# A Delta-net layer and two convolutional FFNs on one core: new prices in the planner, and a second product that runs four places later

## The chip, the core and the metric

The program runs on one core of a Trainium2 chip. The core has a matrix engine (TensorE, PE in the profile; PEld is its weight load), three engines for element-wise work (VectorE = DVE, ScalarE = ACT, GpSimd = POOL), and a sync engine (SyncE = SP) whose queue issues most of the DMA transfers. POOL issues the transfers that add to what lies in memory. The metric is the device time of one execution, in microseconds (us). Each engine and each queue works its instructions in the order in which they stand in the program, and waits where an input is not ready.

## The reference

The model is a residual trunk of two layers on 1024 positions by 1024 channels, float32 throughout.

- Layer 0, attention part: `h = h + gated_deltanet(rmsnorm(h))`. A projection to q, k, v, z and two gates, a causal convolution of four taps with SiLU on q, k, v, then for 8 heads a chunked delta rule: inside a chunk a triangular system is solved, from chunk to chunk a state is carried, so that the chunks of a head follow one another. The output is normalised per head, multiplied with SiLU(z) and projected.
- Layer 1, attention part: chunked softmax attention over a key band, with a learned bias per head.
- After each of them: `h = h + conv_ffn(rmsnorm(h))`, that is

```
h = causal_dwconv(xn @ w_up, conv_w) + conv_b      # 1024 -> 5632 channels, three taps
gate, val = h[..., :2816], h[..., 2816:]
return (silu(gate) * val) @ w_down                 # 2816 -> 1024
```

- A final rmsnorm.

## The kernel before, in words

Every float32 factor of a product is cut into a high part that the PE reads exactly and a low rest (`hi`, `lo`), and a product is three matmuls: hi·hi, hi·lo, lo·hi. ACT copies the high part (`uh`, `dh`, `eh`), POOL or DVE subtracts it for the low part (`ul`, `dl`, `el`). Activations lie with channels on the partitions, 128 at a time, in two halves of 512 positions.

**Delta net (up to some 680 us).** The order in which instructions are emitted comes from a planner, the class `Flow`. It keeps a model of time `wv.T` that advances with each matmul group, and for each of DVE, ACT and POOL the time at which that engine is free: `wv.on("D", 1.3)` says that 1.3 us of work have just been emitted for DVE and returns when it will be done. Each piece of work (`gram`, `prep`, `merge`, `chain`, `finish`, `gate`, `yz`) is a generator that yields the time at which its next matmul can go. When none is due the planner emits an eighth of a dense projection tile (0.69 us in its model). A piece has a rank; among those that are due the lowest goes first, and ranks of 2 and more are held back when DVE or ACT is more than 4 us behind. So the prices in `wv.on` decide where each small matmul stands between the dense ones, and the PE then follows that order and waits where the model was too hopeful. Small tiles of 512 columns that live shortly (`th`, `yo`, `zt`, `sq`, `ez`) share two buffers under the tag `zt`.

**FFN (twice, from some 680 and some 1920 us).** The 22 tiles of the first product (one `val` and one `gate` block of 128 channels each) are made by a scheme with seven products of half-size matrices instead of eight (Strassen's): per tile `j` products 1, 7, 6, 5, 2, 4, 3, each 12 matmuls of 128x512 into a PSUM bank `pu`. Before a product, `left_sum` adds weight blocks (`r<-r,r` on DVE) and `operand` cuts them (`uh`, `ul`) two places ahead; after it, `after` puts the bank into `keep`, `keep7`, `vpre`, `gpre`. Then come three taps of `val` and three of `gate` (`taps`: the first on ACT, L1548; the others on DVE, L1551), `silu`, and `gated` (val times gate). Product 4 adds to the bank of product 7, so it may start only when `keep7` has read that bank.

The second product takes the hidden tiles in nine groups `g` of two, again with seven products (`second`, bank `pd`), whose results are drained into `stage` and added to DRAM by accumulating transfers (`drain`, `send`; one quarter first goes to `d_e`, which `load_e` and `send_e` add to three others at the end). The last four tiles, 18 to 21, are multiplied directly (`pf`), with weights `fr` that `load_last` loads and `cut_last` cuts, from hidden tiles that `hidden` cuts (`hidh`, `hidl`).

All of this stands in one list `seq` of PE steps, here called places. `at(i, f, rank)` puts the work `f` of the other engines ahead of place `i`; within a place, lower ranks come first. `pos[j, s]` is the place of the `s`-th product of tile `j`, `pos["d", g, n]` that of a product of group `g`, `end` the last product of tile 21, and `fin_at` the last product of the last group. When layer 1 finishes, its residual is loaded as `res` (`load_r`) and the sums as `ht` (`load_t`); in layer 0 they are `h`.

The attention between the two FFNs is not touched.

Of the kernel before, what the change touches and what calls it, by code (L numbers as in the profile page):

```python
# [9 lines left out]
F32 = mybir.dt.float32  # L10
# [8 lines left out]
KT = 8  # L19
# [9 lines left out]
def trunk_kernel(  # L29
# [541 lines left out]
    with ExitStack() as ph:  # L571
# [43 lines left out]
        soo, ff, rr = gt("soo"), gt("ff"), gt("rr")  # L615
# [23 lines left out]
        def split_tile(raw):  # L639
            wt = split_w(raw, [P, KT, P])  # L640
            wv.on("A", 1.0)
            return wt
# [24 lines left out]
        def project(m, dsts, key, store=None, n_from=0):  # L667
# [4 lines left out]
            def post(s, ps):  # L672
# [16 lines left out]
                def silu():  # L689
                    th = dp.tile([P, HALF], F32, name="th", tag="zt", bufs=2)  # L690
                    nc.scalar.activation(th, d, AF.Tanh)
                    nc.gpsimd.tensor_scalar(th, th, 1.0, 1.0, op0=ALU.add, op1=ALU.mult)
                    nc.gpsimd.tensor_tensor(d, d, th, op=ALU.mult)
# [44 lines left out]
        def gram(t):  # L738
# [11 lines left out]
            def decay(i):  # L750
                hd, E = hds[i], Es[i]
                nc.vector.tensor_tensor(E, E, negm.rearrange("p (o t) -> p o t", o=1).broadcast_to([P, 4, P]), op=ALU.add)
                yield wv.on("D", 0.75) - wv.slack
# [4 lines left out]
                yield wv.on("A", 1.4)  # L758
# [4 lines left out]
            for i, hd in enumerate(hds):  # L763
# [27 lines left out]
                slot[0] = t_ = wv.on("D", 1.3)  # L791
# [10 lines left out]
            wv.mark(("scale", t), wv.on("D", 1.2))  # L802
# [48 lines left out]
        def invert_blocks(t):  # L851
# [167 lines left out]
        def finish(t, j):  # L1019
# [18 lines left out]
            t_ = wv.on("D", 1.3)  # L1038
# [8 lines left out]
        def turn(k, s, vv):  # L1047
# [5 lines left out]
            yo = dp.tile([P, HALF], F32, name="yo", tag="zt", bufs=2)  # L1053
# [51 lines left out]
        def yz(k, s):  # L1105
# [11 lines left out]
            yield wv.on("D", 0.7) - wv.slack  # L1117
# [4 lines left out]
        def split_yt(yt, s, k):  # L1122
# [6 lines left out]
            wv.mark(("act", k, s), wv.on(e, 0.7 if e == "D" else 1.3, t))  # L1129

        def gate_z(hd):
            def post(s, ps):
                zt = dp.tile([P, HALF], F32, name="zt", tag="zt", bufs=2)
# [48 lines left out]
        def gates(gT):  # L1182
# [9 lines left out]
            ez = dp.tile([P, HALF], F32, name="ez", tag="zt", bufs=2)[:, 0:136].rearrange("p (c j) -> p c j", j=8)  # L1192
# [84 lines left out]
        env["tmp"] = lambda: dp.tile([P, HALF], F32, name="sq", tag="zt", bufs=2)  # L1277
# [28 lines left out]
        def out_tile(m, s):  # L1306
# [19 lines left out]
            def then():  # L1326
# [4 lines left out]
                wv.on("D", 0.65, wv.on("A", 0.65))  # L1331
# [8 lines left out]
            wv.later(wv.on("D", 0.6), then)  # L1340
# [25 lines left out]
        with tc.manual_schedule(engines={mybir.EngineType.PE, mybir.EngineType.DVE, mybir.EngineType.Activation}):  # L1366
# [20 lines left out]
            for n, (k, s) in enumerate([(k, 0) for k in range(8)] + [(k, 1) for k in range(4)]):  # L1387
                wv.add(3, ("yz", n % 6), wv.when(*[("gram", hd, 1) for hd in range(4, 8)]), yz(k, s))
# [29 lines left out]
    def ffn(layer, h, hp, xs, tail, d_r, last):  # L1418
# [215 lines left out]
        for c, (j, n) in enumerate(plan):  # L1634
# [3 lines left out]
            for g in range(NG):  # L1638
                for n, o in zip(ORDER, (2, 3, 5, 6, 8, 9, 11) if g == 0 else (-2, 0, 2, 4, 6, 8, 10)):
# [4 lines left out]
        for i, (j, n) in due.items():  # L1644
# [37 lines left out]
        for j in range(3, FP - 1):  # L1682
# [5 lines left out]
            0: [(11, (g0,), 0), (12, (v0,), 0), (13, (v1,), 2), (13, (v2,), 2.7), (15, (g1, g2, silu), 2), (17, (gated,), 2)],  # L1688
            1: [(18, (v0, v1), 2), (19, (v2, g0), 2), (20, (g1,), 2), (21, (g2, silu), 2), (22, (gated,), 2)],
            2: [(24, (v0, v1), 2), (25, (v2, g0), 2), (26, (g1,), 2), (27, (g2, silu), 2), (28, (gated,), 2)],  # L1690
        }
        for j in range(3, FP - 1):
            when[j] = [(pos[j, 7], (v0, v1), 2), (nx(j, 1), (v2, g0), 2), (nx(j, 2), (g1,), 2)]
            when[j] += [(nx(j, 3), (g2,), 2), (nx(j, 4), (silu,), 1.6), (nx(j, 5), (gated,), 2)]
            if j >= 2 * NG:
                when[j].append(({18: fin_at + 5, 19: fin_at + 7}.get(j, nx(j, 6)), (hidden,), 1.9))
# [135 lines left out]
        last_at = [pos[FP - 1, s] for s in (3, 4, 5, 6)] + [end + 1] * 4  # L1832
        if layer == 1:
            last_at = [pos[FP - 1, 2]] + last_at[:-1]
            last_at[5] = end
            last_at[7] = end + 2
# [21 lines left out]
        for q in range(8):  # L1858
            s = (1, 1, 2, 3, 4, 4, 5, 6)[q]
            at(fin_at + 1 if q < 2 else pos[FP - 1, s], lambda q=q: load_last(q), 1)  # L1860
            at(last_at[q], lambda q=q: cut_last(q), 1.5)

        if layer == 0:
# [55 lines left out]
        else:  # L1919
# [58 lines left out]
            for t in range(4):  # L1978
                step(("f", t, 0), tile_of(t, range(3)))
            for t in range(4):  # L1980
                step(("f", t), tile_of(t, range(3, 4)))
# [431 lines left out]
```

## Time and profile before

| | |
|---|---|
| median of 3 runs | 2588.57 us (2588.05 to 2591.74) |
| the profiled execution, own time | 2588.85 us |
| its span in the profile | 2587.0 us |
| PE busy | 2506.2 us, 13933 matmuls |
| DVE busy | 1861.0 us |
| POOL busy | 1476.3 us |
| ACT busy | 1414.3 us |

The span runs from the first to the last instruction of the program. A row of the view of stretches gives the bounds, the length, then busy time and number of instructions of PE, PEld, DVE, ACT and POOL, the granted PE clock (1.00 is full speed), the share of the 16 DMA engines and their rate. In the timeline a row is start, duration, engine, line, operation, and in brackets the idle time before it and what ended it. In the view of waits a row is the waiting instruction, what it waited for, the total in us, how often and the longest.

### The profile page before, as it was taken

The page shows a single profiled execution, that of the slowest core. Times are in us where ns is not written, and L with a number is a line of the kernel's source. Part 1 is how long each engine was busy: PE and PEld are TensorE (multiplying, and loading weights), DVE is VectorE, ACT ScalarE, POOL GpSimd, SP SyncE. Part 2 cuts the span into 40 slices and gives each one's busy share as a digit, 9 for nine tenths or more (in the row PEclk, how much of TensorE's full clock was granted, in tenths as well). Part 3 has the DMA queues.
Part 4 walks back from the last instruction along what each step waited for, and adds up shares of the span by engine and source line. Part 5 has one row for each costly group of instructions (what it writes and reads, how often), then busy time and mean ns, then how long its engine had stood idle before and what let it go on. Part 6 is the DMA issues. An engine that isn't in the chain of part 4 may idle for free.

```text
span 2587.0 us, 39395 instructions
## 1 busy us (share of the span) xinstructions
PE 2506.2 (97%) x13933; PEld 2068.8 (80%) x13933; DVE 1861.0 (72%) x3102; ACT 1414.3 (55%) x2735; POOL 1476.3 (57%) x1466
## 2 busy tenths in 40 slices
PE   7999999999999999999999999999999999999988
PEld 5878788888877888888788888887876788888877
DVE  5765864554588888888876666666488788888875
ACT  6444455464455555655556555565455655565553
POOL 3655543345437777777726444443433777777770
PEclk9999999999999999999999999999999999999999
DMA  4534435555436777777841211113332576777785
GB/s 128 139 100 118 127 101 161 147 166 156 121 82 135 147 144 153 156 153 152 173 157 54 65 52 56 45 50 100 104 97 79 138 151 143 154 155 150 158 190 174
DMA packets 320598, 325.15 MB, mean 126 GB/s; under 512 B 32912, under 2 KB 244624, under 8 KB 320400
## 3 DMA queue, kind: packets, MB, share of 16 engines
q1 hardware_dynamic: 289584, 219.59, 29.0%
q0 software_dynamic: 25920, 94.38, 20.5%
q10 hardware_dynamic: 4896, 8.65, 1.0%
q8 instruction: 110, 1.80, 0.3%
q14 instruction: 88, 0.72, 0.1%
HBM read 179.89 MB, written 142.67 MB: 125 GB/s over the span
## 4 chain that ended last, share of the span: by engine, by line
PE 54%; DVE 6%; POOL 3%; issue 3%; ACT 2%; DMA 1%; DVEq 0%; ACTq 0%; POOLq 0%
PE pu L1458 8%; PE pu L1456 8%; PE pu L1457 8%; PE pd L1458 4%; PE pd L1457 4%; PE pd L1456 4%; PE acc L119 3%; PE acc L120 3%; PE acc L121 3%; PE ptp L2137 2%; POOL ul L1423 2%; PE sc L2109 1%; PE poT L2167 1%; PE poT L2166 1%; PE sc L2110 1%
## 5 line engine op out<-in xcount | busy, mean ns | idle before, releaser
L1423 POOL TENSOR_TENSOR ul<-r,uh 128x512 fp32r<-128x512 f32 x282 | 445.4, 1598 | 304.9 <-ACT uh L1444 280.9
L119 PE MATMUL acc<-xh,whi 128*128 128x512 f32 x896 | 375.4, 419 | 0.2
L120 PE MATMUL acc<-xl,whi 128*128 128x512 f32 x896 | 354.0, 395 | 2.0 <-POOL xl L421 1.0
L121 PE MATMUL acc<-xh,wlo 128*128 128x512 f32 x896 | 352.7, 394 | 0.0
L1444 ACT CAST uh<-r 128x512 fp32r<-128x512 f32 x296 | 181.7, 623 | 218.0 <-DVE r L1423 176.8
L104 POOL TENSOR_TENSOR wlo<-wraw,whi 128x256 fp32r<-128x256 f32 (+2 forms) x206 | 169.4, 851 | 159.1 <-ACT whi L102 139.3
L1456 PE MATMUL pu<-xh,uh 128*128 128x512 f32 x552 | 216.0, 391 | 2.8 <-ACT uh L1444 1.3
L1458 PE MATMUL pu<-xh,ul 128*128 128x512 f32 x552 | 215.7, 391 | 1.7 <-POOL ul L1423 1.7
L1457 PE MATMUL pu<-xl,uh 128*128 128x512 f32 x552 | 215.5, 390 | 1.0 <-POOL xl L421 1.0
L1778 ACT COPY stage<-pd 128x1024 f32<-128x1024 f32 x180 | 174.8, 1013 | 49.4 <-PE pd L1458 49.4
L121 PEld LDWEIGHTS acc<-xh,wlo 128*128 128x128 f32 x896 | 168.9, 189 | 37.3
L120 PEld LDWEIGHTS acc<-xl,whi 128*128 128x128 f32 x896 | 170.2, 190 | 25.5 <-DVE xl L1163 3.2
L119 PEld LDWEIGHTS acc<-xh,whi 128*128 128x128 f32 x896 | 169.9, 190 | 21.7 <-ACT xh L1162 1.1
L2117 POOL TENSOR_SCALAR sS<-sS,st 128x640 f32<-128x640 f32 (+4 forms) x128 | 85.3, 668 | 172.4 <-DVE st L2116 125.2
L1551 DVE SCALAR_TENSOR_TENSOR val<-vpre,colt,val 128x1023 f32<-128x1023 f32 (+2 forms) x92 | 152.8, 1661 | 38.6 <-ACT val L1548 38.4
L1423 POOL TENSOR_TENSOR dl<-a,dh 128x512 fp32r<-128x512 f32 x90 | 154.7, 1719 | 38.4 <-ACT dh L1444 38.4
L1551 DVE SCALAR_TENSOR_TENSOR gate<-gpre,colt,gate 128x1023 f32<-128x1023 f32 (+2 forms) x92 | 175.1, 1903 | 0.8
L1423 DVE TENSOR_TENSOR r<-r,r 128x512 f32<-128x512 f32 x168 | 131.8, 785 | 31.0 <-POOL ul L1423 29.6
L2115 ACT ACTIVATE sS<-sS,st 128x640 f32<-128x640 f32 (+4 forms) x128 | 89.3, 697 | 101.7 <-DVE st L2114 100.2
L1458 PEld LDWEIGHTS pu<-xh,ul 128*128 128x128 f32 x552 | 103.8, 188 | 26.0 <-POOL ul L1423 4.6
L1456 PEld LDWEIGHTS pu<-xh,uh 128*128 128x128 f32 x552 | 103.9, 188 | 25.3 <-ACT uh L1444 1.8
L1457 PEld LDWEIGHTS pu<-xl,uh 128*128 128x128 f32 x552 | 103.9, 188 | 23.5 <-POOL xl L421 2.1
(401 smaller groups left out, 7158.9 us busy)
## 6 DMA issues: line engine op xcount, KB each, us to landing
r<-in_f_w_up_dram SPq DMA_DIRECT2D x176, 256.0 KB, 4.3
d_r<-stage POOLq DMA_DIRECT2D x78, 512.0 KB, 7.8
d_c<-stage POOLq DMA_DIRECT2D x70, 512.0 KB, 8.1
a<-in_f_w_down_dram SPq DMA_DIRECT2D x72, 256.0 KB, 2.8
wraw<-in_a_w_in_dram SPq DMA_DIRECT2D x32, 512.0 KB, 4.7
d_e<-stage POOLq DMA_DIRECT2D x32, 512.0 KB, 8.9
wraw<-in_a_w_out_dram SPq DMA_DIRECT2D x16, 512.0 KB, 4.0
d_r<-h ACTq DMA_DIRECT2D x32, 256.0 KB, 3.8
```

The costliest lines, as they stand in the source:

```text
L104: nc.gpsimd.tensor_tensor(lo[:, c], raw[:, c], hi[:, c].bitcast(F32), op=ALU.subtract)
L119: mm(ps, hi[:, kw, wcol : wcol + P], rh[k][s], start=st, stop=False)
L120: mm(ps, hi[:, kw, wcol : wcol + P], rl[k][s], start=False, stop=False)
L121: mm(ps, lo[:, kw, wcol : wcol + P], rh[k][s], start=False, stop=sp)
L1423: tt = lambda eng, o, a, b, op: eng.tensor_tensor(o, a, b, op=op)
L1444: copy(hi, src)
L1456: mm(ps, w[0][:, cw], x[0], start=first, stop=False, skip_group_check=True)
L1457: mm(ps, w[0][:, cw], x[1], start=False, stop=False, skip_group_check=True)
L1458: mm(ps, w[1][:, cw], x[0], start=False, stop=last, skip_group_check=True)
L1551: nc.vector.scalar_tensor_tensor(t_[:, a:c1], p_[:, a - step : c1 - step], w[:, 2 - step : 3 - step], t_[:, a:c1], op0=ALU.mult, op1=ALU.add)
L1778: nc.scalar.copy(t_, ps)
L2115: nc.scalar.activation(S, S, AF.Exp, bias=st[:, 1:2], accum_out=st[:, 2:3])
```

## The change

No instruction is added or removed: the built program holds the same instructions on each engine, in another order. The attention part keeps its order. The parts are these.

1. Delta net: the prices in the planner are replaced. The split of a weight tile now also charges POOL (2.75), which it did not; the scaling after `gram` goes from 1.2 to 3.5, the one in `finish` from 1.3 to 2.2, the sums in `gram` from 1.4 to 1.95, the column of the solver from 0.3 + 0.0031 i² to 0.4 + 0.0022 i², others by a tenth or two. The tag `zt` gets a third buffer; to make room, `soo` lies where `gg` lay. `yz` of the first half gets rank 1.5 instead of 3.
2. FFN: the seven products of a group stand 2, 4, 6, 8, 10, 12 and 14 places (of the first product) behind the tile that they follow, in all nine groups. They stood at -2, 0, 2, 4, 6, 8, 10, and in group 0 at 2, 3, 5, 6, 8, 9, 11.
3. FFN ends: with the groups, `fin_at` moves from behind the third product of tile 20 to behind its seventh. The taps of tile 19 start three products later, the last gate taps of tile 20 one later; the hidden tiles 18, 19 and 20 are cut at the fifth, the sixth and behind the seventh product of tile 21 (before: first, third and sixth). The left sum for product 7 of tile 21 is made one place earlier. The three `send_e` of a half no longer stand together. The last product goes over the hidden tiles 18 and 19 for all its outputs, then over 20, then over 21 (before: 18 to 20, then 21). `cut_last` moves.

```
-        soo, ff, rr = gt("soo"), gt("ff"), gt("rr")
+        soo, ff, rr = gg, gt("ff"), gt("rr")
...
-            wv.on("A", 1.0)
+            wv.on("G", 2.75, wv.on("A", 1.0))
...
-                    th = dp.tile([P, HALF], F32, name="th", tag="zt", bufs=2)
+                    th = dp.tile([P, HALF], F32, name="th", tag="zt", bufs=3)
...
-                wv.on("D", 1.4)
+                wv.on("D", 1.95)
...
-            wv.mark(("scale", t), wv.on("D", 1.2))
+            wv.mark(("scale", t), wv.on("D", 3.5))
...
-                t_ = wv.on("D", 0.3 + 3.1e-3 * i * i)
+                t_ = wv.on("D", 0.4 + 2.2e-3 * i * i)
...
-            t_ = wv.on("D", 1.3)
+            t_ = wv.on("D", 2.2)
...
-                wv.add(3, ("yz", n % 6), wv.when(*[("gram", hd, 1) for hd in range(4, 8)]), yz(k, s))
+                wv.add(1.5 if s == 0 else 3, ("yz", n % 6), wv.when(*[("gram", hd, 1) for hd in range(4, 8)]), yz(k, s))
...
-                for n, o in zip(ORDER, (2, 3, 5, 6, 8, 9, 11) if g == 0 else (-2, 0, 2, 4, 6, 8, 10)):
+                for n, o in zip(ORDER, (2, 4, 6, 8, 10, 12, 14)):
...
+                if j == FP - 1 and n == 1:
+                    at(i - 2, lambda j=j: left_sum(j, 7), 1.05)
...
+            late_ = 1 if j == FP - 2 else 0
+            if j == FP - 3:
+                q_ = [pos[j + 1, 3], pos[j + 1, 4], pos[j + 1, 5], pos[j + 1, 6], pos[j + 1, 7]]
+                when[j] = [(q_[0], (v0, v1), 2), (q_[1], (v2, g0), 2), (q_[2], (g1, g2), 1.3), (q_[3], (silu,), 1.6), (q_[4], (gated,), 2), (pos[FP - 1, 6], (hidden,), 1.9)]
+                continue
...
-                when[j].append(({18: fin_at + 5, 19: fin_at + 7}.get(j, nx(j, 6)), (hidden,), 1.9))
+                when[j].append(({18: fin_at + 5, 19: pos[FP - 1, 5], 20: end + 1}[j], (hidden,), 1.9))
...
-            for k, n in enumerate((6, 7, 4)):
-                at(i + 2 + k // 2, lambda u=u, n=n: send_e(u, n), 0.6)
+            for n, (k, r) in zip((6, 7, 4), ((2, 0.6), (2, 2.9), (3, 2.9)) if u == 0 else ((2, 2.9), (3, 2.9), (4, 2.9))):
+                at(i + k, lambda u=u, n=n: send_e(u, n), r)
...
-            at(last_at[q], lambda q=q: cut_last(q), 1.5)
+            at(last_at[q], lambda q=q: cut_last(q), 0.9 if layer == 0 else 1.5)
...
-            for m in range(KT):
-                step(("f", 0, m, 0), part(0, m, range(3)))
-            for m in range(KT):
-                step(("f", 0, m), part(0, m, range(3, 4)))
+            for i, ks in enumerate((range(2), range(2, 3), range(3, 4))):
+                for m in range(KT):
+                    step(("f", 0, m, i) if i < 2 else ("f", 0, m), part(0, m, ks))
```

More of the change, by code (lines that the diff above doesn't have):

```diff
@@ L1052, in turn @@
             wv.pe(4, 0.11)
-            yo = dp.tile([P, HALF], F32, name="yo", tag="zt", bufs=2)
+            yo = dp.tile([P, HALF], F32, name="yo", tag="zt", bufs=3)
             nc.scalar.activation(yo, po, AF.Copy, scale=g_o)
@@ L1190, in bc8 @@
                 return r.rearrange("p (o j) -> p o j", o=1).broadcast_to([P, 8, 8])
-            ez = dp.tile([P, HALF], F32, name="ez", tag="zt", bufs=2)[:, 0:136].rearrange("p (c j) -> p c j", j=8)
+            ez = dp.tile([P, HALF], F32, name="ez", tag="zt", bufs=3)[:, 0:136].rearrange("p (c j) -> p c j", j=8)
             nc.vector.tensor_copy(ez[:, 16], alog)
@@ L1275, in trunk_kernel @@
         d_us = [dram.tile([4, 4, 4, 32, 32], F32, name=f"d_u{t}") for t in range(4)]
-        env["tmp"] = lambda: dp.tile([P, HALF], F32, name="sq", tag="zt", bufs=2)
+        env["tmp"] = lambda: dp.tile([P, HALF], F32, name="sq", tag="zt", bufs=3)
         env["run"] = lambda s: late.tile([P, HALF], F32, name="run", tag="run", bufs=1)
@@ L1338, in then @@
                         wv.add(1, "normed", lambda: t0 + 0.5, tail(its[s]))
-            wv.later(wv.on("D", 0.6), then)
+            wv.later(wv.on("D", 0.7), then)
             yield
@@ L1831, in ffn @@
         slots = [(k, 1) for k in range(4)] + [(k, 1) for k in range(4, 8)] if layer == 0 else [(k, 0) for k in range(4)] + [(k, 1) for k in range(4)]
[L1832 to L1836, printed above, removed]
+        last_at = [pos[FP - 1, s] for s in (3, 4, 5, 6)] + ([end, end, end + 1, end + 1], [end + 1, end + 1, end + 3, end + 3])[layer]
         def load_last(q):
@@ L1976, in closing @@
                 return f
[L1978 to L1981, printed above, removed]
+            for i, ks in enumerate((range(2), range(2, 3), range(3, 4))):
+                for t in range(4):
+                    step(("f", t, i) if i < 2 else ("f", t), tile_of(t, ks))
             for t in range(4, KT):
```

22 lines of the change are left out of this document (11 added, 11 removed).

## The prediction

> **What bounds the kernel now.** I read the busy shares first, then the PE's time by stretches, then the view of PE waits for each stretch that lost time, and last the timeline of the engine that was waited for.
>
> ```profile
> PE 2506.2 (97%) x13933; PEld 2068.8 (80%) x13933; DVE 1861.0 (72%) x3102; ACT 1414.3 (55%) x2735; POOL 1476.3 (57%) x1466
> ```
> ```profile
> 40.00:680.00 640.00, 620.36 (x5017) 518.66 (x5016) 375.96 (x981) 314.70 (x851) 317.53 (x425) 1.00 0.47 134
> ...
> 752.00:804.00 52.00, 48.10 (x198) 35.92 (x197) 43.98 (x41) 30.34 (x44) 33.41 (x25) 1.00 0.50 114
> 804.00:1230.00 426.00, 425.53 (x1868) 349.79 (x1867) 361.03 (x335) 251.62 (x357) 330.98 (x245) 1.00 0.73 151
> 1230.00:1300.00 70.00, 65.54 (x279) 52.81 (x278) 56.85 (x52) 35.89 (x53) 49.21 (x37) 0.98 0.83 185
> ...
> 1970.00:2024.00 54.00, 50.58 (x213) 39.00 (x212) 43.12 (x42) 29.84 (x43) 28.45 (x19) 1.00 0.29 98
> 2024.00:2460.00 436.00, 435.68 (x1914) 358.44 (x1914) 364.76 (x343) 257.96 (x366) 337.52 (x248) 1.00 0.71 150
> 2460.00:2530.00 70.00, 63.42 (x262) 50.13 (x262) 55.45 (x51) 34.88 (x51) 49.57 (x38) 0.95 0.90 209
> ```
>
> PE is the bound: busy 97%, and the change keeps its 13933 matmuls. So the time can fall only by what PE stands idle or runs at half clock, and rises only by new idling. The rows give the idle time (length less PE busy) where the change reaches: 19.6 us in the Delta net, 3.9 and 3.4 where the second product begins in each FFN, 0.5 and 0.3 in their long middles, 4.5 and 6.6 at their ends. The other idle stretches (the start, the first tiles of each FFN, the attention, the final norm) are not reached. A middle shows the pace: 1868 matmuls in 426 us are 0.228 us each, so a place of 12 matmuls takes 2.74 us, and two tiles with their group (21 places) 57.5 us.
>
> Half clock costs as well:
>
> ```profile
> 301.00:304.40 3.40, 3.40 (x11) 2.70 (x11) 2.59 (x4) 1.78 (x3) 3.39 (x6) 0.50 0.00 0
> ...
> 1290.80:1294.30 3.50, 3.50 (x10) 2.71 (x9) 3.00 (x2) 1.46 (x3) 2.72 (x2) 0.51 0.83 243
> ...
> 2519.60:2526.50 6.90, 6.23 (x15) 4.92 (x16) 6.90 (x7) 4.05 (x7) 4.46 (x3) 0.51 0.68 191
> ```
>
> Three stretches granted 0.5: half of 3.4 and 3.5 us is 1.7 each; of the third, half of its 6.23 us busy, less some 0.2 at its edges, is 2.9. Each comes right after one of the longest PE waits below (2.5, 3.4 and 3.4 us).
>
> **Part 1, the Delta net: -6.7 us.** What PE waited for between 40 and 680 us:
>
> ```profile
> PE pq L721 <- POOL kq L693: 5.0, 3, 2.3
> PE pc L992 <- DVE S L1011: 3.6, 4, 2.3
> PE po L1051 <- POOL vv L1041: 2.5, 1, 2.5
> ...
> PE pm L911 <- DVE T L907: 1.8, 2, 1.3
> ```
> ```profile
> 126.33 2.83 POOL L104 TENSOR_TENSOR wlo<-wraw,whi 128x256 fp32r<-128x256 f32 x4 [0.80 <-ACT whi L102]
> ```
> ```profile
> 263.22 0.17 DVE L607 TENSOR_SCALAR sk<-ssk 128x16 int32<-128x16 int32 x1
> ...
> 267.81 0.18 DVE L801 TENSOR_TENSOR sk<-sk,ssk 128x16 f32<-128x16 f32 x1
> ```
> ```profile
> 296.21 0.16 DVE L1034 TENSOR_SCALAR ff<-ssq 128x8 f32<-128x8 f32 x1
> ...
> 298.74 0.17 DVE L612 SCALAR_TENSOR_TENSOR rr<-t,rr 128x8 f32<-128x8 f32 x1
> ```
> ```profile
> 298.98 2.06 POOL L1041 TENSOR_TENSOR vv<-vv,rr 128x512 f32<-128x512 f32 x2 [8.69 <-DVE rr L612]
> ```
> ```profile
> 300.09 0.65 PE L1051 MATMUL po<-ident,vv 128*128 128x128 f32 x4 [2.54 <-POOL vv L1041]
> ```
>
> These waits are errors of the planner's prices. The scaling behind `gram` ran from 263.22 to 267.99, 4.8 us, and was priced 1.2 (now 3.5); the one in `finish` from 296.21 to 298.91, 2.7 us, priced 1.3 (now 2.2); the POOL work of a weight split took 2.83 us and had no price (now 2.75). With the old prices the planner sent `po` while `vv` was still behind the first of these: the 2.54 us wait and the half clock after it. With the new ones the small matmuls stand further back, with dense ones in front. The four rows of waits sum to 12.9 us. Other waits there (DMA, ACT copies) are not addressed. A new order mends some and makes some: between all of it (-12.9, and -1.7 for the clock) and none, with as much new waiting as the addressed sort has now in a third of the stage (+4.3), I take two thirds mended (-8.6), the clock (-1.7), and +3.6 of new waits, near the lower row sums: -6.7.
>
> The third `zt` buffer and `soo` in `gg`'s place cost nothing: no instruction is added, and `gg` is last read by two matmuls before 60 us, long before `soo` is written. If it brings something it is in the `kq` row. The rank of `yz` moves the loads of `yt` and `zt` on SP's queue earlier; what stands behind them there are weight loads for a tile that is 16 places of 0.69 us away, which cover it. In the built order the dense tiles still fill the stage to its end: 45 matmuls of 512 columns (10.3 us) stand between the last turn of a head and the first output tile that needs it (75 before), over three element-wise steps, so the margin shrinks but holds.
>
> **Part 2, the groups four places later and group 0 spread: -4 us.** Waits of 752 to 804 us:
>
> ```profile
> PE pu L1458 <- POOL ul L1423: 1.6, 3, 0.7
> PE pu L1456 <- ACT uh L1444: 1.1, 2, 0.7
> ```
>
> Here seven products of group 0 stand among nine of the first one, with the taps of tiles 1 and 2 beside them, so that DVE's sums for the next operand come late, and `uh` and `ul` with them. Spread over 13, with group 1 also four later, each place has less DVE work. The idle 3.9 and 3.4 sum to 7.3; between all and nothing I take a little over half, -4. The silu of tiles 0 and 2 one place later sits on ACT between copies and changes nothing: its tile is used three places on.
>
> In the middles a group's work meets other taps than before. PE idles there 0.5 and 0.3 us now. By the built order the densest run of places before is two drains and a `val` tap, a `val` tap, four sums, two drains and a `gate` tap in a row; afterwards the drains stand alone in their places. I take 0. The 72 loads of `w_down` blocks on SP and the accumulating sends on POOL's queue go with their groups; behind a send on POOL stands the next `ul`, as before.
>
> **Part 3, the ends: -11.2 us.** Waits of 2460 to 2530 us; the stretch 1230 to 1300 has the same first and last row:
>
> ```profile
> PE pu L1456 <- DVE keep L1423: 3.4, 1, 3.4
> PE pu L1456 <- ACT uh L1444: 1.3, 1, 1.3
> PE pu L1458 <- POOL ul L1423: 1.0, 2, 0.6
> PE pd L1456 <- ACT stage L1778: 0.9, 1, 0.9
> ```
>
> In the first FFN, DVE ahead of the late `keep`:
>
> ```profile
> 1281.89 1.77 DVE L1423 TENSOR_TENSOR fl<-fr,fh 128x512 fp32r<-128x512 f32 x1
> 1283.59 2.31 DVE L1423 TENSOR_TENSOR hidl<-val,hidh 128x1024 fp32r<-128x1024 f32 x1
> 1285.82 2.29 DVE L1551 SCALAR_TENSOR_TENSOR gate<-gpre,colt,gate 128x1022 f32<-128x1022 f32 x1
> 1288.03 1.41 DVE L1423 TENSOR_TENSOR keep<-pu,keep 128x512 f32<-128x512 f32 x2
> ```
>
> Product 4 of tile 21 waits for this `keep`. Both `hidl` that stood before it (18 and 19) now come after it, and the last gate tap too: 2.31 + 2.29 us leave DVE's queue in the last two places alone, against 3.4 of waiting. So both waits go (3.4 each) with their half clocks (1.7 and 2.9): -11.4. In the second FFN the waits for `uh` and `ul` hang on a load:
>
> ```profile
> r<-in_f_w_up_dram SPq DMA_DIRECT2D x176, 256.0 KB, 4.3
> ```
> ```profile
> 2496.20 0.39 SPq L1502 DMA_DIRECT2D r<-in_f_w_up_dram  x1
> 2496.64 14.68 SPq L1936 DMA_DIRECT2D res<-d_r  x4
> ```
> ```profile
> 2496.20 15.97 DMA r<-in_f_w_up_dram
> ```
>
> The last weight block took 15.97 us instead of 4.3, amid `res` loads and accumulating sends. Now the `res` loads follow `fin_at` to behind it: -2.3. The two `stage` waits (0.9 each) I leave as they are.
>
> Against it: tile 19's gate taps now run in one place of tile 20, and ACT may write `gpre` of tile 20 only behind them, with the `uh` of a coming product queued behind that on ACT.
>
> ```profile
> L1551 DVE SCALAR_TENSOR_TENSOR gate<-gpre,colt,gate 128x1023 f32<-128x1023 f32 x42 | 54.6, 1299 | 0.0
> L1551 DVE SCALAR_TENSOR_TENSOR gate<-gpre,colt,gate 128x1022 f32<-128x1022 f32 x42 | 114.5, 2727 | 0.7
> ```
>
> They take 4.0 us in a place of 2.74, so 1.3 late; between 0 and 2.5, I take 1.25 in each FFN: +2.5. Sum: -11.4 - 2.3 + 2.5 = -11.2.
>
> Costed at nothing, with their cover: `hidl` of 18 and 19 now stand between `keep` and the last product. From the executed `keep` to its start are four places less 1.4, 9.6 us; DVE has a sum, a gate tap, `vpre`, an `fl` and the two `hidl` there, 8 us, or 10.4 at the slow durations above, 0.8 too much. Tile 20's is needed only behind the first pass, 10.9 us later. `send_e` and the loads of `fr`, `res` and `ht` come closer to the end: `ht` is used 27 us behind the sixth product of tile 21, and 16 loads of 0.7 us behind a last send of 8 us take 19.
>
> **Sum.** -6.7 - 4 - 11.2 = -21.9: the profiled execution, 2588.85 us with a span of 2587.0, would take 2566.9. Its own time is 0.3 above the median of 2588.57, so the median would be 2566.7, rounded 2567.
>
> **Rivals.**
> - *Slower: the new phase stalls in the middles.* Sums, taps and cuts meet in other places; if one operand per two tiles came late in each of the 15 periods, the price is a PE wait each. It decides from 21.9 / 15 = 1.5 us. Half of group 0's idle now (3.7 / 2 = 1.8 us) times 15 is +27.8: 2594. For it: DVE 85% and POOL 78% busy in the middles. Against: the present phase, with denser places, loses 0.5 us in 426.
> - *No gain: the waits only move.* The planner's new order waits elsewhere (+6.7), and `hidl`, `fr` and `ht` hold the PE before the last products for what `keep` did (+11 with clock): 2585 to 2588. For it: the work of the ends is the same and DMA is busy 0.90 there. Against: the margins above.
> - *A smaller gain:* the ends give half (5.6) and the Delta net nothing: 2588.6 - 4 - 5.6 = 2579.
> - *The half clocks stay.* They would not hang on these waits but come by themselves. For it: there are waits of 2.3 us in the Delta net without one. Then 1.7 + 1.7 + 2.9 = 6.3 of the gain is lost: 2573. The Trainium skill ("TensorE: Matmul & The Clock Gate", section on what is actually happening) lets the clock fall to half after an idle window of about 3.4 us, on windows that run freely. Taken to the letter, waits of 2.5 us would cause none; the trace has one right behind 2.54 us, so mostly idle seems enough, and the waits stay the likely cause.
> - *More:* all addressed waits and clocks go: 14.6 + 7.3 + 15.5 = 37: 2551.
>
> **How the numbers follow.** The forecast, 2558 to 2576, has 0.50; the half clocks 0.08; the smaller gain 0.14; more than forecast 0.10; no gain 0.10; slower 0.08. The measurement can tell 0.2%, 5.2 us, from no change: faster ends at 2583.4, slower begins at 2593.7. The first four cases lie on the faster side, 0.82, less 0.02 for a smaller gain that misses the bound: 0.80. No gain and that 0.02 are same, 0.12, and slower has 0.08. The range leaves one in ten at either side: from 2551, where all goes, to 2588, where nothing does.
>
> **What would show it.** Part 1: the waits for `kq`, `S`, `vv` and `T` between 40 and 680 us below half of 12.9, and no 0.5 clock near 300. Part 2: the stretch where group 0 begins idle below 2 us in each FFN, the middles below 1. Part 3: no wait for `keep`, clock 1.0 in the last tile, the last `r` load landing in under 8 us. It would be wrong if new waits appear before the first `pf` (hidden tiles or `res` late), at tile 20 for `uh` behind `gpre`, or evenly in the middles.

## The result, and the profile after

The changed kernel takes 2679.87 us (median; 2678.9 to 2680.35) against 2589.47 us: a ratio of 1.0348, 95% interval 1.033 to 1.0366. It is slower by 90 us where 22 us less were forecast. The profiled execution has a span of 2678.3 us.

I first cut both traces at the same work: the start of the first product of each group of the second product in each FFN, group 8's last matmul, and the end of the last product (`pf`). Four places of first products (4 x 2.74 = 10.96 us) that now stand ahead of group 1 and no longer behind group 8 are taken out of the differences.

| stretch | before, us | after, us | difference for equal work |
| --- | --- | --- | --- |
| start to group 0, first FFN | 751.42 | 746.02 | -5.4 |
| group 0 to group 1, first / second FFN | 53.73 / 52.30 | 66.28 / 64.83 | +1.6 / +1.6 |
| group 1 to group 8 (seven periods of two tiles) | 402.40 / 401.82 | 441.87 / 440.66 | +39.5 / +38.8 |
| group 8 to its last matmul | 53.48 / 53.32 | 60.40 / 58.84 | +6.9 / +5.5 |
| that to the end of the last product | 81.69 / 91.29 | 76.64 / 76.62 | +5.9 / -3.7 |
| from there to group 0 of the second FFN (with the attention) | 638.59 | 639.14 | +0.5 |

The sum is 91.2 us, and the spans differ by 91.3. Nearly all of it, 90.7, lies in the periods of groups 1 to 8, which the prediction had put at nothing. One of them now takes 63.1 us instead of 57.5. The view by windows shows that stretch of the first FFN (length, then busy time and instructions of PE, its weight loads, DVE, ACT and POOL, then clock), before:

```profile
805.15:1207.55 402.40, 401.98 (x1766) 330.60 (x1764) 341.48 (x315) 237.37 (x336) 314.60 (x234) 1.00 0.72 148
```

and after:

```profile
812.30:1254.17 441.87, 413.60 (x1765) 327.54 (x1764) 355.89 (x316) 235.44 (x337) 316.44 (x233) 1.00 0.67 134
```

The work is the same, the clock is 1.00 in both, and DMA is less busy than before: neither the clock nor transfers made this. PE's idle time grew from 0.4 to 28.3 us; the other 11.6 us of the loss stand in its busy time, for the same matmuls. A matmul takes 0.39 us in the record and the next one usually starts 0.23 us behind it, so the first part of a gap does not show as idle time: around a wait listed with 1.61 us (976.15) the starts are 2.01 and 0.34 us apart. The waits below are therefore somewhat too short.

The view of PE's waits (total, times, longest) has no row for this stretch of before. After, it has these (in the second FFN 15.8 and 9.9 us):

```profile
PE pu L1458 <- POOL ul L1423: 15.9, 28, 0.9
PE pd L1457 <- POOL el L1423: 11.5, 7, 1.7
...
```

That is four `ul` and one `el` a period, seven times over. GpSimd computes both, and over the stretch it is busy for 316 of 442 us; who holds it is found one engine back at a time. Of DVE's waits in the same stretch this row grew most, before and then after:

```profile
DVE val L1551 <- ACT val L1548: 9.2, 7, 1.3
```
```profile
DVE val L1551 <- ACT val L1548: 31.0, 14, 3.1
```

VectorE's second `val` tap waits for the first one, which ScalarE does. Before, it waited at one tile of two; now it waits at both, and 3.1 us at one. The timelines of the three engines at that tile, changed kernel (start, duration, engine, instruction, and the idle time before it with its releaser):

```profile
955.91 0.69 DVE L1423 TENSOR_TENSOR vpre<-pu,keep 128x512 f32<-128x512 f32 x1 [0.48 <-PE pu L1458]
956.52 2.73 DVE L1423 TENSOR_TENSOR ay<-ay,a 128x512 f32<-128x512 f32 x1
...
963.64 1.28 DVE L1551 SCALAR_TENSOR_TENSOR val<-vpre,colt,val 128x1023 f32<-128x1023 f32 x1 [3.06 <-ACT val L1548]
...
965.44 0.68 DVE L1423 TENSOR_TENSOR r<-r,r 128x512 f32<-128x512 f32 x1
```
```profile
960.01 0.62 ACT L1444 CAST dh<-a 128x512 fp32r<-128x512 f32 x1 [3.15 <-DVE a L1423]
960.54 1.92 ACT L1785 COPY stage<-pd 128x1024 f32<-128x1024 f32 x2
962.35 1.25 ACT L1548 ACTIVATE val<-vpre,colt 128x1024 f32<-128x1024 f32 x1
```
```profile
966.89 1.55 POOL L1423 TENSOR_TENSOR ul<-r,uh 128x512 fp32r<-128x512 f32 x1 [4.89 <-ACT uh L1444]
969.90 1.75 POOL L1423 TENSOR_TENSOR ul<-r,uh 128x512 fp32r<-128x512 f32 x1 [1.46 <-ACT uh L1444]
971.62 2.28 POOL L1423 TENSOR_TENSOR dl<-ay,dh 128x512 fp32r<-128x512 f32 x1
973.85 2.25 POOL L1423 TENSOR_TENSOR el<-val,eh 128x512 fp32r<-128x512 f32 x1
```

`vpre` is there at 956.6, but ScalarE's first tap starts at 962.35: ahead of it on ScalarE's queue stand the cast `dh`, which waits for VectorE's sum `a` (late in part because the sum `ay` ahead of it took 2.73 us instead of 0.68, see the last section), and the two copies that drain product 5 of the group (1.92 us). VectorE's tap waits for it, and behind that tap are queued `gpre` and the sum `r` for the next tile's product 7. So `r` comes at 965.44, 9.5 us behind the start of `vpre`. ScalarE's cast, GpSimd's `ul` (idle for 4.89 us until then) and all that follows on GpSimd, down to `el`, are late with it. At the same tile before, the drain in this place was that of product 6, on VectorE:

```profile
895.81 0.69 DVE L1423 TENSOR_TENSOR vpre<-pu,keep 128x512 f32<-128x512 f32 x1 [2.25 <-PE pu L1458]
...
898.50 2.34 DVE L1423 TENSOR_TENSOR stage<-pd,stage 128x1024 f32<-128x1024 f32 x2
900.76 1.57 DVE L1551 SCALAR_TENSOR_TENSOR val<-vpre,colt,val 128x1023 f32<-128x1023 f32 x1
...
902.86 0.67 DVE L1423 TENSOR_TENSOR r<-r,r 128x512 f32<-128x512 f32 x1
```
```profile
899.14 1.24 ACT L1548 ACTIVATE val<-vpre,colt 128x1024 f32<-128x1024 f32 x1
```

ScalarE did the first tap while VectorE did the additions, no tap waited, and `r` came 7.05 us behind `vpre`. At the other tile of the period the additions of product 7 now stand ahead of `vpre` on VectorE, and its tap waits 1.4 us:

```profile
926.65 2.34 DVE L1423 TENSOR_TENSOR stage<-pd,stage 128x1024 f32<-128x1024 f32 x2
928.91 0.68 DVE L1423 TENSOR_TENSOR vpre<-pu,keep 128x512 f32<-128x512 f32 x1
930.96 1.61 DVE L1551 SCALAR_TENSOR_TENSOR val<-vpre,colt,val 128x1023 f32<-128x1023 f32 x1 [1.38 <-ACT val L1548]
```

So the theory is a head-of-line block: in a queue that works in order, an instruction that cannot start yet holds up all that stands behind it. Shifted by four places, a drain stands in a queue ahead of what the `val` taps need. Its rivals: another edit starves the middles; GpSimd is full where `el` and `ul` are late; VectorE has no room in this phase; the new phase is short of lead everywhere.

### The profile page after: what moved, and what is told of

Read it like the earlier page. It is cut to its first block, busy times and chain, and to the rows that moved or that the text cites. A ratio compares the mean times of both kernels' runs of the same rounds, so it can differ in the third digit from the quotient of the medians.

```text
span 2678.3 us, 39353 instructions
## 1 busy us (share of the span) xinstructions
PE 2536.3 (95%) x13933; PEld 2066.0 (77%) x13933; DVE 1890.9 (71%) x3102; ACT 1411.4 (53%) x2735; POOL 1476.4 (55%) x1466
## 4 chain that ended last, share of the span: by engine, by line
PE 52%; POOL 19%; issue 15%; DVE 9%; ACT 3%; DMA 2%; SPq 0%; POOLq 0%; DVEq 0%; ACTq 0%
POOL ul L1423 9%; PE acc L119 6%; PE acc L120 6%; PE acc L121 6%; POOL dl L1423 4%; PE pu L1458 3%; PE pu L1456 3%; PE pu L1457 3%; PE acco L119 2%; PE acco L120 2%; PE acco L121 2%; PE ptp L2138 2%; POOL el L1423 2%; PE pd L1458 1%; PE pd L1457 1%
## 5 line engine op out<-in xcount | busy, mean ns | idle before, releaser
L1551 DVE SCALAR_TENSOR_TENSOR val<-vpre,colt,val 128x1023 f32<-128x1023 f32 (+2 forms) x92 | 141.8, 1541 | 94.6 <-ACT val L1548 94.4
L1423 DVE TENSOR_TENSOR r<-r,r 128x512 f32<-128x512 f32 x168 | 165.4, 984 | 38.9 <-POOL ul L1423 37.5
L1551 DVE SCALAR_TENSOR_TENSOR gate<-gpre,colt,gate 128x1023 f32<-128x1023 f32 (+2 forms) x92 | 167.0, 1815 | 0.8
L1423 DVE TENSOR_TENSOR el<-val,eh 128x512 fp32r<-128x512 f32 x90 | 88.4, 982 | 73.4 <-ACT eh L1444 73.4
```

Source lines behind the costliest of these rows:

```text
L1423: tt = lambda eng, o, a, b, op: eng.tensor_tensor(o, a, b, op=op)
L1551: nc.vector.scalar_tensor_tensor(t_[:, a:c1], p_[:, a - step : c1 - step], w[:, 2 - step : 3 - step], t_[:, a:c1], op0=ALU.mult, op1=ALU.add)
```

## The experiments

"Period" is the mean from group 1 to group 8 of the first FFN in the run's trace; the ratio is to the kernel before, run beside it.

| kernel | time, us | ratio (95%) | period, us |
| --- | --- | --- | --- |
| changed | 2679.9 | 1.0348 (1.033 to 1.0366) | 63.1 |
| e1: groups at their old places | 2585.5 | 0.9978 (0.9968 to 0.9987) | 57.5 |
| e3: drain of product 5 behind the taps | 2649.8 | 1.0222 (1.0207 to 1.0237) | 61.3 |
| e4: Delta net's edits alone | 2584.4 | 0.9969 (0.9957 to 0.998) | 57.5 |
| e6: `el` of 6 and 7 on VectorE | 2698.8 | 1.0412 (1.0396 to 1.0427) | 64.4 |
| e7: e3, `el` of 5 and 3 on GpSimd, not 6 and 7 | 2718.3 | 1.0482 (1.0465 to 1.0499) | 65.5 |
| e8: e3, drain of product 7 behind `vpre` | 2621.3 | 1.0109 (1.0092 to 1.0126) | 59.7 |
| e9: e7 and e8 together | 2683.5 | 1.0354 (1.0337 to 1.0371) | 63.9 |
| e11: e8, `el` of 6 alone on VectorE | 2624.8 | 1.0125 (1.0107 to 1.0143) | 60.1 |
| e13: e1 with copies put ahead of the taps | 2598.8 | 1.0022 (1.0012 to 1.0033) | 58.6 |
| e10: e1, other PSUM banks in the first end | 2588.3 | 0.9992 (0.9983 to 1.0001) | 57.5 |
| e12: e1, the first end as before | 2581.6 | 0.9959 (0.9943 to 0.9975) | 57.5 |

**The shift alone (e1).**

```diff
-                for n, o in zip(ORDER, (2, 4, 6, 8, 10, 12, 14)):
+                for n, o in zip(ORDER, (2, 3, 5, 6, 8, 9, 11) if g == 0 else (-2, 0, 2, 4, 6, 8, 10)):
```

> The changed kernel with one edit taken back: the groups of the second product stand where they stood before (group 0 at its old places, the others four places earlier). The two middles of the changed kernel lost 39.5 and 38.8 us against before from the start of group 1 to the start of group 8, and group 8 6.9 and 5.5 more. Theory 'the shift itself' (the new phase of groups against tiles makes the loss): a period of two tiles falls back from 63 to 57.5 us and the time to 2576 to 2588 (2679.9 less 90.7 and 3.2, with the ends open by 10). Rival 'the other edits' (moved taps, the new order of the Delta net or the ends starve the middles): the periods stay at 63 and the time above 2650.

Measured 2585.5 and a period of 57.5; PE's waits in the stretch are 0.5 us in all. The loss belongs to where the groups stand, not to the moved taps, the Delta net or the ends by themselves. What is left of the change is a gain of 0.2%.

**The drain of product 5 (e3).**

```diff
-                at(p_[n] + 1, lambda g=g, n=n: drain(g, n), 0)
+                at(p_[n] + 1, lambda g=g, n=n: drain(g, n), 2.2 if n == 5 else 0)
```

> The changed kernel with one rank moved: the two ScalarE copies that drain a group's third product (n=5) stand behind the taps of their place, not ahead of them. In the changed kernel VectorE's second val tap waits 3.1 us for ScalarE's first val tap there (1.3 at the other tile), ScalarE's first tap stands behind the two copies (1.9 us), and the sums r for the next two products are queued behind the waiting tap. Theory 'head of line': the wait falls to some 1.2, the sums come 1.9 us earlier, the PE wait of 1.65 us for the low part el and that of 0.9 for ul in the same cluster go, a period falls from 63 to about 60.5 to 61.3, and the time to 2637 to 2653 (15.5 periods by 1.75 to 2.7). Rival 'GpSimd is full there' (three subtractions in one place, el on GpSimd among them): its waits stay, time above 2670.

Nothing is removed; two ScalarE copies go behind two taps in the same place. The time falls by 30 us to 2649.8. VectorE's longest wait for the tap is 1.4 us instead of 3.1 (first fence), and PE's wait for `ul` halves, while that for `el` stays:

```profile
DVE val L1551 <- ACT val L1548: 18.3, 14, 1.4
```

```profile
PE pd L1457 <- POOL el L1423: 11.5, 7, 1.7
PE pu L1458 <- POOL ul L1423: 8.4, 14, 0.7
```

At the tile shown above `r` now comes 7.75 us behind `vpre` (958.63 and 950.88), 1.78 us earlier than in the changed kernel, and the period is shorter by the same 1.78 (61.34 against 63.12). So the block is shown; that the wait for `el` would go with it was wrong.

**The drain of product 7 (e8, on e3).**

```diff
-                at(p_[n] + 1, lambda g=g, n=n: drain(g, n), 2.2 if n == 5 else 0)
+                at(p_[n] + (2 if n == 7 else 1), lambda g=g, n=n: drain(g, n), {5: 2.2, 7: 0.1}.get(n, 0))
...
-                    at(p_[n] + 2, lambda g=g, n=n: send(g, n), 0.5)
+                    at(p_[n] + (3 if n == 7 else 2), lambda g=g, n=n: send(g, n), 0.5)
```

> The kernel with the third product's drain behind the taps (2649.8 us), and the two VectorE additions that drain product 7 (2.3 us) stand one place later, behind vpre, with their sends a place later too. In the changed kernel they stand ahead of vpre; ScalarE's first tap waits for vpre, VectorE's second tap waits 1.4 us for that, and the sum r for product 7 of the next tile comes behind; PE then waits for two ul, 0.5 and 0.85 us. Theory 'head of line' for this tile too: the tap's wait of 1.4 goes (the additions fill it), PE's two waits go, a period falls from 61.3 to about 60, time 2625 to 2635. Rival 'it only moves': product 4 waits for its bank, or ul stays late for GpSimd's sake: 2645 or more.

Another 28.5 us less: 2621.3. PE's waits for `ul`, 15.9 us in the changed kernel and 8.4 in e3, are down to 1.0; what is left is `el`:

```profile
PE pd L1457 <- POOL el L1423: 11.6, 7, 1.7
PE pu L1458 <- POOL ul L1423: 1.0, 6, 0.2
```

**What is left: `el` on GpSimd (e6, e7, e9, e11).** The line below decides which `el` GpSimd computes. e6 starts from the changed kernel, e11 from e8; e7 (on e3) and e9 (on e8) have `n == 5` there and send the `el` of product 3 to GpSimd too:

```diff
-            cut_low(src, *bops[g, n], nc.gpsimd if n in (6, 7) else nc.vector)   # e6: nc.vector
+            cut_low(src, *bops[g, n], nc.gpsimd if n == 7 else nc.vector)        # e11
```

> The changed kernel with the low parts el of products 6 and 7 computed on VectorE as those of the others, not on GpSimd. Theory 'GpSimd is full there': the PE wait for el (11.5 us in 7 periods of the first FFN) and most of that for ul (17.3) go, a period falls to 58 to 60 us, time 2590 to 2630. Theory 'head of line': el is no longer late by GpSimd's queue, so its 1.65 us a period goes, but VectorE's tap still waits 3.1 us for ScalarE and ul stays late: period 61 to 62.5, time 2645 to 2670.

> The kernel with the third product's drain behind the taps (2649.8 us, 61.3 us a period), and the two low parts el that GpSimd computes per group are now those of products 5 and 3, with those of 6 and 7 on VectorE: against the tiles they stand where they stood in the kernel before. What is left of the loss there is a PE wait of 1.66 us a period for el, which on GpSimd stands behind ul (1.75) and dl (2.28), and 1.35 us for two ul at the other tile. Theory 'GpSimd's queue at that place': the wait for el goes, a period falls to 59.5 to 60, time 2622 to 2632. Rival 'VectorE has no room there': the sums behind el come later instead, new waits for stage or ul, a period of 61 or more, time 2645 or more (with both low parts simply moved to VectorE the time had risen by 19).

> All three edits on the changed kernel: drain of the third product behind the taps, drain of product 7 behind vpre, low parts of 5 and 3 on GpSimd instead of 6 and 7. If the loss of the new phase is these three collisions and nothing else, the period comes back to 58.0 to 58.7 us (57.5 before) and the time to 2595 to 2612. If the phase loses by something general (less lead for every operand, transfers), it stays above 2630.

> The kernel with both drains moved behind (2621.3 us) and the low part el of product 6 alone on VectorE, that of 7 still on GpSimd. What is left there is one PE wait of 1.65 us a period for el on GpSimd, behind ul (1.75) and dl (2.24). Theory 'GpSimd's queue at that place': the wait goes, a period falls from 59.7 to 57.7 to 58.2, time 2595 to 2603, and nothing else is left of the loss. Rival 'VectorE has no room' (moving el of 6 and 7 to VectorE had cost 19 us, and putting those of 5 and 3 in their stead on GpSimd 69): the additions of stage or the next sums come later, time 2621 or more.

In all four PE's wait for `el` is gone, and none is faster than the kernel it starts from: e6 is slower by 19 us, e7 by 68, e9 by 62 (against e8), and e11 cannot be told from e8 (1.0125 and 1.0109, with intervals that overlap). What PE waits for in its stead, in e7 and then in e11:

```profile
PE pu L1458 <- POOL ul L1423: 14.7, 32, 0.7
PE pd L1456 <- ACT stage L1785: 8.2, 7, 1.2
PE pd L1456 <- DVE stage L1423: 8.2, 7, 1.5
```
```profile
PE pd L1456 <- DVE stage L1423: 12.2, 7, 1.8
PE pu L1458 <- POOL ul L1423: 3.1, 7, 0.5
```

So "GpSimd is full there", as the cause, falls. My hope that three collisions were all did not come true either, but e9 does not settle it, because its third edit brought new waits of its own. Taken off GpSimd, `el` makes VectorE's drain late. Why VectorE has no room there shows in e11's timelines, VectorE and then GpSimd:

```profile
971.74 5.91 DVE L1423 TENSOR_TENSOR val<-val,gate 128x1024 f32<-128x1024 f32 x1
```
```profile
972.14 3.17 POOL L1423 TENSOR_TENSOR ul<-r,uh 128x512 fp32r<-128x512 f32 x2
974.65 1.90 POOL L1423 TENSOR_TENSOR dl<-a,dh 128x512 fp32r<-128x512 f32 x1
```

A product that takes 1.21 us elsewhere lasts until 977.65, 1.1 us after the last of three GpSimd subtractions ends (976.55): it stood still beside them. The same comes one period earlier (5.90 us at 911.54); in e8 the product at that place took 3.15 us. The two additions that PE then waits for stand behind it on VectorE. Of the new phase's 5.6 us a period, 1.8 are product 5's drain (63.1 to 61.3) and 1.6 product 7's (61.3 to 59.7). The last 2.2 (59.7 against 57.5) stay open: most of them show as the wait for `el` (1.65 a period), but no kernel tried here removed them.

**The block put into the good phase (e13, on e1).**

```diff
-                    tt(nc.vector, t_, ps, t_, add)
+                    if n == 6 and g:
+                        nc.scalar.copy(t_, ps)
+                    else:
+                        tt(nc.vector, t_, ps, t_, add)
```

> The collision put into the good phase: the changed kernel with the groups at their old places (2585.5 us), where the drain of product 6, two VectorE additions (2.4 us) in the place of the first val tap of one tile in two, becomes two ScalarE copies (1.9 us) in the same place, from group 1 on. The addition of two products is left out, so VectorE has 2.4 us less a period to do. Theory 'head of line' (copies ahead of the first tap hold VectorE's second tap and all sums behind it): in spite of less work a period rises from 57.5 to 58 to 59.5, the tap waits 2 to 3 us, PE waits for ul or el, time 2592 to 2612. Rival 'VectorE's load decides': a period stays at 57.5 or less, time 2580 to 2587.

e13 leaves out the two additions. VectorE has 2.4 us less to do a period, and the period still rises from 57.5 to 58.6, the time from 2585.5 to 2598.8. VectorE's wait for the tap grew as in the changed kernel:

```profile
DVE val L1551 <- ACT val L1548: 34.8, 14, 3.7
```

Against "VectorE's load decides", this shows the block from the other side. ScalarE has 1.9 us more to do a period, which this run alone cannot tell from the place of the copies; e3 moves copies without adding any. PE's wait rows for the stretch hold only 2.6 us, though the stretch took 7.5 us more than in e1; here too part of the loss does not show as idle time of PE.

**The Delta net alone (e4)** is the kernel before with the part of the diff ahead of the FFN's plan.

> The kernel before with the edits of the Delta net alone (prices, third zt buffer, soo in gg's place, rank of yz). The first product of group 0 began 5.4 us earlier in the changed kernel than before. Theory 'the Delta net gave 5.4': 2583 (2581 to 2585). Rival 'it gave nothing and the spread of group 0 shows in that difference': 2587 to 2590.

2584.4, a ratio of 0.9969: the Delta net's part pays, by 7.4 us (5 to 11).

**The ends (e10, e12, both on e1).** e10 changes the banks in which the first FFN's last product is summed; e12 takes the whole of the first FFN's new end back.

```diff
-                        if s == 0 and m > 3:
+                        if s == 0 and m < 4:
...
-                    at(pos["f", s, m | 1 if s == 0 and m > 3 else m] + 1, closing(s, m), 0)
+                    at(pos["f", s, m | 1 if s == 0 and m < 4 else m] + 1, closing(s, m), 0)
```

> The changed kernel with the groups at their old places (2585.5 us), and in the first FFN's last product the first four tiles of the output take the two double PSUM banks and the last four the single ones, which are released only when vpre and gpre of tile 21 have been read. In the run with old places PE waited there 0.67 us for vpre and 2.03 for gpre, and the granted clock was 0.94 in the last 53 us. Theory 'banks': both waits go, with some or all of the clock: 2580 to 2583. Rival 'the operands hidl or fl are late there anyway': 2584 to 2588.

> The changed kernel with the groups at their old places (2585.5 us) and the end of the first FFN as before; so the Delta net's edits and the new end of the second FFN alone. In the profile of the run with old places the new end of the first FFN lost 5 us against before (start of group 8 to the last product), that of the second gained 6.5. Theory 'the ends differ': 2585.5 less 5: 2579 to 2582, faster than before by 0.35 to 0.5%. Rival 'the two ends differ only by what one execution varies': 2584 to 2588.

In the first end, e1 had these waits (first fence). In e10 those for `gpre` and `vpre` are gone and a longer one has come, for the additions `h` that free the banks (second fence):

```profile
PE pf L1456 <- DVE gpre L1423: 2.0, 1, 2.0
PE pu L1456 <- DVE keep L1423: 1.9, 1, 1.9
...
PE pf L1456 <- DVE vpre L1423: 0.7, 1, 0.7
```
```profile
PE pf L1456 <- DVE h L1423: 6.6, 1, 6.6
```

So e10 fell. e12 is the fastest kernel here, 2581.6 us, 0.41% under the kernel before (0.25 to 0.57%). It has the Delta net's edits and the second FFN's new end, and neither the shift nor the first FFN's new end. Its interval overlaps those of e4 and e1, so what each end adds is read from the traces and not from these times: from the start of group 8 to the last product's end, e1 took 140.3 us in the first FFN and 138.1 in the second, against 135.2 and 144.6 before. The traces of e4 (both old ends: 135.4 and 143.0) and e12 (136.6 and 138.1) agree: the new end of the first FFN costs 4 to 5 us, that of the second brings 5 to 6.5.

## Why the prediction was wrong, point by point

**Part 2, the middles: "I take 0" is the step that failed.** It measured +90.7 us, of which 3.4 belong to part 3 (below). The argument behind it counted work per place, and on VectorE only: "afterwards the drains stand alone in their places" held for VectorE's additions and not for ScalarE's copies. Those of product 5 came to stand ahead of ScalarE's first `val` tap. The three engines are one loop (sum on VectorE, cast on ScalarE, subtraction on GpSimd, next sum), each takes its instructions in order, and a drain that waits for PE, or stands behind a cast that waits, delays the whole loop. Even alone in their place, the additions of product 7 held up `vpre` and the tap at the other tile. e3 and e8 show it by moving drains only; e13, which puts copies in, agrees. Together e3 and e8 take back 3.4 of the 5.6 us a period; what makes the other 2.2 was not found.

**The rival "new phase stalls in the middles" is what happened, and it was under-priced.** It had a chance of 0.08 at 1.8 us a period; the price was 5.6 (39.5 / 7). Half of group 0's idle time has nothing to do with it: what prices such a loop is the delay handed on. At one tile `r` comes 2.5 us later behind `vpre` than before (9.53 against 7.05); where e3 took 1.78 of this back, the period fell by 1.78. At the other tile VectorE's tap waits 1.4 us; where e8 took that away, the period fell by 1.6. The point from which it decides, 1.5 us, was the whole forecast gain over 15 periods. All other rows together came to +0.5 in the traces, so any loss in the middles would have made this kernel slower.

**Part 2, group 0: -4 forecast, +3.2 measured** (1.6 in each FFN). Spread over 13 places, its later products stand in the shifted phase, so the same waits came. The spread by itself, without the shift, was not tried.

**Part 1, the Delta net: -6.7 forecast, -5.4 in the trace and -7.4 by e4.** The size was right, the terms only in part. PE idle between 40 and 680 us fell from 19.6 to 12.8 (first fence). The addressed waits went from 12.9 to 2.5, more than the two thirds I took. New ones came on a weight split and on a load, 6.4 us and so more than the 3.6 allowed, and others that I had not counted on went; that all waits not addressed rose by only 3.5 (6.9 to 10.4) was luck.

```profile
40.00:680.00 640.00, 627.19 (x5051) 526.59 (x5050) 373.27 (x984) 317.41 (x855) 322.74 (x428) 0.99 0.48 136
```
```profile
PE acc L121 <- POOL wlo L104: 3.2, 1, 3.2
PE pv L844 <- DMA vv<-d_v: 3.2, 1, 3.2
PE pq L721 <- POOL kq L693: 2.5, 1, 2.5
```

And the -1.7 for the half clock near 300 failed: in the changed kernel one stands behind the first of these waits, below, and another behind the second (0.53 from 503.0 to 506.4).

```profile
311.60:315.00 3.40, 2.99 (x7) 2.37 (x8) 0.32 (x1) 0.00 (x0) 3.32 (x6) 0.50 0.21 77
```

**Part 3, the ends: -11.2 forecast, +2.2 in the changed kernel** from group 8's last matmul on. Without the shift (e1) they measured +5.1 and -6.5 from the start of group 8. The two waits for `keep` (3.4) did not go; they became 1.9 and 1.8 there, and 1.6 each in the changed kernel. Both `hidl` left the queue ahead of `keep`, as said, but I had priced what stays there at its usual duration. It stands still beside GpSimd's subtractions: in e1 a gate tap of 5.25 us (1.27 elsewhere; first fence), in the changed kernel an `fl` of 7.05 (0.68 elsewhere; second fence), both in the first FFN; the second has 5.24 and 6.50.

```profile
1276.42 5.25 DVE L1551 SCALAR_TENSOR_TENSOR gate<-gpre,colt,gate 128x1023 f32<-128x1023 f32 x1
1281.59 1.40 DVE L1423 TENSOR_TENSOR keep<-pu,keep 128x512 f32<-128x512 f32 x2
```
```profile
1321.78 7.05 DVE L1423 TENSOR_TENSOR fl<-fr,fh 128x512 fp32r<-128x512 f32 x1 [1.42 <-ACT fh L1857]
```

In the second FFN's end the last `r` load of the changed kernel landed in 3.1 us instead of 15.97 (first fence), as said; in e1 the wait for `uh` is gone, and beside `keep` (1.8) only that for `ul` is left, at 1.0 as before (second fence).

```profile
r<-in_f_w_up_dram SPq DMA_DIRECT2D x1, 256.0 KB, 3.1
```
```profile
PE pu L1458 <- POOL ul L1423: 1.0, 2, 0.6
```

In the first FFN the shorter first pass over the last product (two tiles of channels instead of three) reaches the single banks sooner, and waits until `vpre` and `gpre` of tile 21 have been read; e10, with other banks there, has neither wait. I had no term for PSUM banks at all. The half clock moved there with the wait: e1 is granted 1.00 from 1254 to 1289 us, around `keep`, and 0.94 from 1289 to 1342.

The +2.5 for tile 19's gate taps came true in the changed kernel, by the path that was named: VectorE's two gate taps end at 1305.4, ScalarE's `gpre` waits for them, and `uh` is queued behind `gpre`. PE waits 1.7 us for this `uh` in each FFN, 3.4 in sum:

```profile
1305.54 0.59 ACT L1593 COPY gpre<-pu 128x512 f32<-128x512 f32 x1 [6.56 <-DVE gate L1551]
1306.03 0.62 ACT L1444 CAST uh<-r 128x512 fp32r<-128x512 f32 x1
```
```profile
PE pu L1456 <- ACT uh L1444: 1.7, 1, 1.7
```

These waits lie ahead of group 8's last matmul, and so among the 90.7 above. Neither end of e1 has them.

The signs that I had named told it: "evenly in the middles" is where nearly all of it was, and "at tile 20 for `uh` behind `gpre`" came too.

## What to carry over

When the phase between two interleaved streams is moved, list for each place what each in-order queue holds ahead of the instruction that the next operand hangs on, ScalarE's copies too; equal work per place says little. Price a late operand in a loop over several engines by the delay that it hands on, times the periods (in e3 1.78 us of delay were 1.78 us a period), and not by the idle time seen now. Beside GpSimd, do not price VectorE work with two SBUF inputs at its usual duration. An edit of fifteen equal periods deserves its own run apart from edits that are paid once.

## What the runs showed of the hardware

A VectorE instruction with two SBUF inputs can stand still beside GpSimd's subtractions: 5.91 us instead of 1.21 in e11 and 7.05 instead of 0.68 for the `fl` above, and 2.73 instead of 0.68 for the sum `ay` in the changed kernel (956.52) beside two `ul`. The additions of `stage`, which read one input from PSUM, never did: all 72 of the changed kernel took 1205 to 1219 ns. In e11 two of them took the usual 2.35 us from 968.27 on, beside a `dl` (968.49) and an `el` (969.76).

```profile
L1423 DVE TENSOR_TENSOR stage<-pd,stage x72: 1205/1209/1219, 790.1 to 2591.3; 128x1024 f32<-128x1024 f32 x72
```

The Trainium skill ("SBUF — State Buffer", section "Who interferes with whom") says that a VectorE instruction with two SBUF inputs contends with a GpSimd instruction that reads SBUF, that the shared port pair is an exclusive lock, and that the order of issue decides who blocks. The traces agree with the contention, and with a block rather than a sharing. They do not bear out the order: in e11 the VectorE instruction is recorded as starting first (971.74 against 972.14), and still it ended behind three GpSimd subtractions in a row. The recorded times of GpSimd are rough, so this is not certain.

The half clock came behind shorter waits than I had thought. In the changed kernel PE waited twice between 776 and 779 us (first fence), and the next 3.4 us were granted half (second fence):

```profile
PE pu L1456 <- ACT uh L1444: 1.1, 1, 1.1
PE pu L1458 <- POOL ul L1423: 0.9, 1, 0.9
```
```profile
779.30:782.70 3.40, 3.40 (x9) 2.61 (x9) 3.37 (x4) 2.77 (x5) 2.25 (x2) 0.51 0.00 0
```

Waits of up to 1.7 us in each of the seven periods that follow left the clock at 1.00. The pair of waits at tile 20, 1.7 us for `uh` and 0.6 for `ul`, came in both FFNs: behind it the clock was 0.51 in the first (1308.4 to 1311.8) and 1.00 in the second (2589.8 to 2593.2). So the length of the waits does not tell by itself whether a half clock follows. The Trainium skill ("TensorE: Matmul & The Clock Gate", section "What's actually happening") lets the clock fall after an idle window of about 3.4 us; none of these waits is that long, and the trace has half clocks none the less.
